# The modulation's three parts beside the first layer's attention: float32 products in four column groups of TensorE in place of sums on VectorE

## The chip, the core and the metric

The kernel runs on one core of one Trainium2 chip. Each run gives one device time in microseconds (us); the metric is that time, and 1309.29 us is the median of three runs before the change (1306.78 to 1309.57). A profile comes from one execution of its own, which took 1307.82 us; its span, from the first to the last instruction, is 1306.0 us. In the rows of the profile PE is TensorE's matmuls, PEld its weight loads, DVE is VectorE, ACT is ScalarE, POOL is GpSimd and SP is SyncE, which issues nearly all DMAs here.

## The reference

A decoder trunk of two layers over 512 positions of width 1024, all in float32. Each layer begins with a modulation: one row of 6144 numbers, the product of a conditioning vector of 1024 with a matrix of 1024 x 6144, plus a bias. It is split into six parts of 1024.

```
c_act = jax.nn.silu(c)
for i in range(DEPTH):
    mod = jnp.einsum('bd,dm->bm', c_act, w_mod[i]) + b_mod[i]
    sh_a, sc_a, gt_a, sh_f, sc_f, gt_f = jnp.split(mod, N_MOD, axis=-1)
    h = modulate(rmsnorm(x, g_mix_pre[i]), sh_a, sc_a)
    qkv = jnp.einsum('bsd,de->bse', h, w_qkv[i])
    ...
    o = jnp.einsum('bse,ed->bsd', merge_heads(o), w_o[i])
    x = x + gt_a[:, None, :] * rmsnorm(o, g_mix_post[i])
    h = modulate(rmsnorm(x, g_ffn_pre[i]), sh_f, sc_f)
    ...
    x = x + gt_f[:, None, :] * rmsnorm(y, g_ffn_post[i])
```

`modulate(h, shift, scale)` is `h * (1 + scale) + shift`; what is left out is the attention (stick-breaking in layer 0, forgetting in layer 1) and the gated MLP with its convolution. The change concerns three parts of layer 0: `gt_a` (in the code `GT_A`), `sc_f` (`SC_F`) and `sh_f` (`SH_F`). None is needed before the attention of layer 0 has ended.

## The kernel before

**Products.** TensorE's products of the model take fp32r operands, to which a float32 is rounded. To keep the precision, a helper splits each operand into a rounded high half and the rest (`split`, L191 to L193: a copy on ACT, a subtraction on DVE or POOL), and each product of the model is three matmuls: high x high, high x low, low x high (`mm3`, L264 to L268). Transpositions (L319, L422) are matmuls of plain float32 against an identity matrix, whose tile is named `zid`.

**The stages.** `begin` makes `sh_a` and `sc_a` of layer 0, normalises the input and makes the first projections, to about 72 us. Then `attention` runs over 16 heads and one round more. For each head TensorE makes four blocks of scores (`ps`, L388), ACT takes two sigmoids of each (L397, L398), DVE makes a running product (`om`, L399), DVE or POOL a product (`bt`, L400), TensorE transposes the result one head later (`pa`, L422), ACT and DVE split it (`ah`, `al`, L192, L193), and TensorE multiplies it by the values (`po`, L437, L438). Between these steps `fill` puts matmuls of the next heads' projections (`pqk`, `pv`), so many per head as the table `UNITS` says. After it comes the output projection with `postnorm`, which needs `GT_A`, and then the gated MLP with `SC_F` and `SH_F`.

**The order of the work.** TensorE and SP keep the order in which the program is written. DVE, ACT and POOL, after `begin`, are ordered by a scheduler before the run; on the chip every engine then works strictly in its order. SP runs ahead of the others and stops only where a buffer that a DMA is to fill is still in use.

**The three parts.** `mod_part` (L130) is a generator that `Background.step` advances a piece at a time; `attention` calls it at the end of each head from the third on, three pieces each (L567), with a priority that lets the scheduler place them early. For one part it loads eight blocks of 128 rows x 1024 columns of the matrix (`wm`, L139) and adds each on DVE, times the conditioning number of its row, to a sum of 128 x 1024 (`acc`; the first by L141, the others by L143, eight by L143 in `GT_A`, whose sum starts from the bias). The sum over the 128 rows is then made on TensorE: `acc` is split (L146, L148) and multiplied by a matrix of ones in four matmuls (L160, L161). For `GT_A` the result is multiplied by a weight vector (L163); for `SC_F` and `SH_F` the diagonal is taken out as columns by eight reductions on DVE (`diagonal`, L128). The conditioning vector lies in `csil`, 128 x 8.

The loads of `wm` go to three buffers of the tag `t4`, shared with other tiles of that size. `xn` is a tag with two buffers, used in `begin` and after the attention. PSUM has eight banks, all of one tag.

Of the kernel before, what the change touches and what calls it, by code (L numbers as in the profile page):

```python
# [8 lines left out]
F32 = mybir.dt.float32  # L9
# [3 lines left out]
ALU = mybir.AluOpType  # L13
AX = mybir.AxisListType

P = 128
D = 1024
S = 512
NT = S // P
ND = D // P  # L20
# [13 lines left out]
SH_A, SC_A, GT_A, SH_F, SC_F, GT_F = range(6)  # L34
# [3 lines left out]
def trunk(ctx, tc, x, c, w_mod, b_mod, g_mix_pre, g_mix_post, w_qkv, w_o, w_fg, b_fg,  # L38
          g_ffn_pre, g_ffn_post, w_gate, w_up, w_conv, b_conv, w_down, out):
    nc = tc.nc  # L40
    cst = ctx.enter_context(tc.tile_pool(name="cst", bufs=1))
    sb = ctx.enter_context(tc.tile_pool(name="sb", bufs=1))
# [4 lines left out]
    def nm(s):  # L47
        serial[0] += 1
        return f"{s}_{serial[0]}"

    def bank(s="b"):
        return pp.tile([P, 512], F32, tag="bank", name=nm(s), bufs=8)

    def slot(s, dt=F32R):
        return sb.tile([P, 512], dt, tag="slot", name=nm(s), bufs=NS)

    def t2(s):
        return sb.tile([P, 512], F32, tag="t2", name=nm(s), bufs=4)

    def t4(s, dt=F32):  # L60
        return sb.tile([P, D], dt, tag="t4", name=nm(s), bufs=3)
# [10 lines left out]
    idn = zid[:, S - P :]  # L72
# [3 lines left out]
    ones = cst.tile([P, P], F32R, name="ones")  # L76
# [9 lines left out]
    colB = [cst.tile([P, 88], F32, name=f"colB{l}") for l in range(DEPTH)]  # L86
    xs = cst.tile([P, NT, D], F32, name="xs")
    csil = cst.tile([P, ND], F32, name="csil")
    rowsA, rowsB, rowsC = t2("rowsA"), t2("rowsB"), t2("rowsC")
    nc.sync.dma_start(rowsC[:ND, :P], c.rearrange("b (r p) -> (b r) p", p=P))  # L90
    nc.scalar.dma_start(rowsA[:96, :P], b_mod.rearrange("l (r p) -> (l r) p", p=P))
# [3 lines left out]
    def b_col(l, comp):  # L95
        return colA[:, 48 * l + 8 * comp : 48 * l + 8 * comp + 8]

    def g_col(l, comp):
        o = (96 if comp == SC_A else 112) + 8 * l
        return colA[:, o : o + 8]  # L100

    def mod_columns():
        ps = bank("pcol")
        nc.tensor.transpose(ps[:, :ND], rowsC[:ND, :P], idn[:ND, :ND])
        nc.scalar.activation(csil, ps[:, :ND], AF.Sigmoid)
        nc.vector.tensor_tensor(csil, csil, ps[:, :ND], op=ALU.mult)
        nc.tensor.transpose(ps[:, 128:256], rowsA[:, :P], idn)
        nc.scalar.copy(colA, ps[:, 128:256])

# [14 lines left out]
    made = {}  # L124

    def diagonal(dst, src):

        nc.vector.tensor_tensor_reduce(junk(P), src, idn, 1.0, 0.0, op0=ALU.mult, op1=ALU.add, accum_out=dst)  # L128

    def mod_part(l, comp):  # L130
        row = comp in (GT_A, GT_F)
        acc = sb.tile([P, D], F32, tag="acc", name=nm("acc"), bufs=1)
        lo_c = comp * D
        if row:
            nc.gpsimd.memset(acc, 0.0)
            nc.sync.dma_start(acc[0:1, :], b_mod[l : l + 1, lo_c : lo_c + D])
        for d in range(ND):
            w = t4("wm")
            nc.sync.dma_start(w, w_mod[l, d * P : (d + 1) * P, lo_c : lo_c + D])  # L139
            if d == 0 and not row:  # L140
                nc.vector.tensor_scalar(acc, w, csil[:, 0:1], None, op0=ALU.mult)  # L141
            else:
                nc.vector.scalar_tensor_tensor(acc, w, csil[:, d : d + 1], acc, op0=ALU.mult, op1=ALU.add)  # L143
            yield
        ah = t4("ah", F32R)
        nc.scalar.copy(ah, acc)  # L146
        al = t4("al", F32R)
        nc.vector.tensor_tensor(al, acc, ah.bitcast(F32), op=ALU.subtract)  # L148
        if row:
            res = sb.tile([P, D], F32, tag="gt", name=nm("gt"), bufs=2)  # L150
            gp = t4("gp")
            g = (g_mix_post if comp == GT_A else g_ffn_post)[l]
            nc.sync.dma_start(gp, g.rearrange("(o n) -> o n", o=1).to_broadcast([P, D]))
        else:
            res = cst.tile([P, ND], F32, name=nm("mc"))
        yield
        for h in range(2):
            cs = slice(512 * h, 512 * h + 512)
            ps = bank("pm")
            nc.tensor.matmul(ps, ones, ah[:, cs], start=True, stop=False)  # L160
            nc.tensor.matmul(ps, ones, al[:, cs], start=False, stop=True)  # L161
            if row:
                nc.vector.tensor_tensor(res[:, cs], ps, gp[:, cs], op=ALU.mult)  # L163
            else:
                for j in range(4):
                    diagonal(res[:, 4 * h + j : 4 * h + j + 1], ps[:, j * P : (j + 1) * P])
            yield
        if not row:
            nc.vector.tensor_tensor(res, res, b_col(l, comp), op=ALU.add)
            if comp in (SC_A, SC_F):  # L170
                nc.vector.scalar_tensor_tensor(res, res, 1.0, g_col(l, comp), op0=ALU.add, op1=ALU.mult)
        made[l, comp] = res

    class Background:
        def __init__(self, parts):
            self.gens = [mod_part(*p) for p in parts]

        def step(self, n=1):
            while n and self.gens:
# [11 lines left out]
    def split(hi, lo, src, engine=None):  # L191
        nc.scalar.copy(hi, src)  # L192
        (engine or nc.vector).tensor_tensor(lo, src, hi.bitcast(F32), op=ALU.subtract)  # L193
# [189 lines left out]
    def scores(l, hd, qb, q, k):  # L383
        n = (qb + 1) * P
        qs = slice(qb * P, n)
        ps = bank("ps")
        for i in range(2):
            nc.tensor.matmul(ps[:, :n], q[hd][:, qs], k[hd][i][:, :n], start=i == 0, stop=i == 1)  # L388
        return ps, n
# [25 lines left out]
    def transposed(probs):  # L415

        res = {}
        for kb in range(NT):
            n = (NT - kb) * P
            ps = bank("pa")  # L420
            for qb in range(NT - 1, kb - 1, -1):
                nc.tensor.transpose(ps[:, (qb - kb) * P : (qb - kb + 1) * P], probs[qb][:, kb * P : (kb + 1) * P], idn)  # L422
            if kb == 1:
                shared = slot("ah"), slot("al")
            hi, lo = (slot("ah"), slot("al")) if kb in (0, 2) else shared
            o = 384 if kb == 3 else 0
            hi, lo = hi[:, o : o + n], lo[:, o : o + n]
            split(hi, lo, ps[:, :n])
            res[kb] = (hi, lo)
            yield res  # L430
# [92 lines left out]
    def drain(g):  # L523
        for _ in g:
            pass

    def attention(l, qk, vt, ot, filler, units, bg):


        get = cums_of.get(l)  # L530
        late, cums = None, {}
        for h in range(NH + 1):
            p, hd = divmod(h, 2)
            done = [0, 0]

            def fill(n=1):
                done[0] += n
                u = (units[h] * min(done[0], 12) + 11) // 12 - done[1]
                done[1] += u
                filler.run(u)  # L540

            if h < NH and hd == 0:
                ot.append((slot("oh"), slot("ol"), slot("of", F32)))
            if get and h < NH:
                for i in range(h, min(h + 2, NH)):
                    if i not in cums:
                        cums[i] = get(i)
            probs, at = {}, None
            turned = transposed(late[0]) if late else None
            for qb in range(NT - 1, -1, -1):  # L550
                if h < NH:
                    ps, n = scores(l, hd, qb, qk[p, 0], qk[p, 1])
                    probs[qb] = stick(ps, n) if l % 2 == 0 else fox(ps, qb, cums[h])
                    fill()
                if turned:
                    at = next(turned)
                    fill()
            fill(2)
            if late:
                drain(turned)  # L560
                for i, _ in enumerate(weighted(late[1], vt, at, ot[late[1] // 2])):
                    if i % 2:
                        fill()
            fill(12)
            late = (probs, h)
            with tc.high_priority(offset=-100):
                bg.step(3 if h > 1 else 0)  # L567


    def begin(vt, qk):  # L570
# [192 lines left out]

    cums_of = {}
    for l in range(DEPTH):
        bg = Background([(l, GT_A), (l, SC_F), (l, SH_F)] if l == 0 else [])
        scale = -0.125 if l % 2 else 0.125
        vt, qk, kl[:] = {}, {}, low_rooms()
        if l == 0:
# [38 lines left out]
        gens += [project(t, ps_) for ps_ in (range(3), range(3, 5)) for t in range(2)] + [project(2, range(3))]  # L808
        filler = Filler(gens)
        attention(l, qk, vt, ot, filler, UNITS[l], bg)  # L810
        filler.finish()
        bg.finish()
# [3 lines left out]
        xn = {}  # L816
# [22 lines left out]
        bg = Background([(l, GT_F)] + ([(l + 1, c_) for c_ in (SC_A, SH_A, SC_F, SH_F, GT_A)] if l + 1 < DEPTH else []))  # L839
# [33 lines left out]
        for f in range(2, NF):  # L873
            g, u = bank("pgu"), bank("pgu")
# [67 lines left out]
```

## Time and profile before

| | |
|---|---|
| median of three runs | 1309.29 us |
| the profiled execution, its span | 1307.82 us, 1306.0 us |
| TensorE's granted clock, mean | 0.989 |
| busy: PE, PEld, DVE, ACT, POOL | 1249.1, 1050.2, 818.9, 620.0, 277.2 us |
| first scores of layer 0, last weighted sum of its attention | 71.9 us, 271.3 us |
| DMAs of `wm` in the attention | 24 of 512 KB, 4.4 us to landing each |

A row of a stage (a window) gives the stretch, its length, the busy time of each engine with its number of instructions, the granted clock, the mean share of the DMA engines and GB/s. A row of a group gives line, engine, operation, the tile written and those read, the shapes and the count; then busy time and the mean of one in ns; then the idle time of the engine just before them and what ended it. The busy time of PE is made of matmuls that overlap, so it is not their cost: that is the distance between one start and the next.

### The profile page before, as it was taken

The numbers are of one execution on the slowest core, as the hardware profiler recorded it, in microseconds if no ns is written. First come the engines' busy times: TensorE is split into PE (matmuls) and PEld (weight loads), VectorE is DVE, ScalarE is ACT, GpSimd is POOL, SyncE is SP. The second block draws the span as 40 slices with busy tenths as digits, with TensorE's granted clock in tenths as the row PEclk, the third lists the DMA queues.
The fourth block names the chain that finished last, engine by engine and source line by source line (L and its number), as shares of the span: only waits on it lengthen the run. The fifth ranks groups of instructions, "written<-read, shape, count | busy, mean of one in ns | idle before, by whom it ended". The sixth has DMA issues, their size and how long they took to land.

```text
span 1306.0 us, 17087 instructions
## 1 busy us (share of the span) xinstructions
PE 1249.1 (96%) x6244; PEld 1050.2 (80%) x6244; DVE 818.9 (63%) x1447; ACT 620.0 (47%) x1182; POOL 277.2 (21%) x302
## 2 busy tenths in 40 slices
PE   5898988999999999999999899999999999999997
PEld 3676867789888888888887788887898888888886
DVE  7778888856878887422264776886775444443233
ACT  5576665757433333311365565566753333332121
POOL 3665444530000000000114554443100000000000
PEclk8999989999999999999999999999999999999999
DMA  8662534231577776333503423232263333333331
GB/s 265 208 193 82 168 107 133 94 108 43 189 242 242 246 229 202 97 97 97 164 1 115 130 91 120 81 129 81 66 210 113 97 97 98 97 97 97 97 97 65
DMA packets 174856, 169.19 MB, mean 130 GB/s; under 512 B 6936, under 2 KB 151728, under 8 KB 174772
## 3 DMA queue, kind: packets, MB, share of 16 engines
q1 hardware_dynamic: 174596, 168.04, 41.1%
q8 instruction: 49, 0.80, 0.3%
q14 instruction: 35, 0.29, 0.1%
q10 hardware_dynamic: 176, 0.07, 0.0%
HBM read 165.92 MB, written 2.16 MB: 129 GB/s over the span
## 4 chain that ended last, share of the span: by engine, by line
PE 72%; DVE 14%; ACT 5%; DMA 4%; issue 3%; POOL 1%; SPq 0%; DVEq 0%; POOLq 0%; ACTq 0%
PE pgu L267 11%; PE pgu L268 11%; PE pgu L266 11%; PE pd L268 6%; PE pd L267 6%; PE pd L266 6%; PE pqk L266 2%; DVE acc L143 2%; PE pqk L267 2%; PE pqk L268 2%; PE po L266 2%; PE po L268 2%; PE po L267 2%; PE ps L388 2%; DMA wm<-in_w_mod_dram 2%
## 5 line engine op out<-in xcount | busy, mean ns | idle before, releaser
L192 ACT CAST wh<-wf 128x1024 fp32r<-128x1024 f32 (+2 forms) x178 | 185.3, 1041 | 319.7 <-PE pgu L267 144.0
L193 DVE TENSOR_TENSOR wl<-wf,wh 128x1024 fp32r<-128x1024 f32 x122 | 149.3, 1224 | 217.9 <-ACT wh L192 215.7
L267 PE MATMUL pgu<-htl,wh 128*128 128x512 f32 (+1 forms) x736 | 276.4, 375 | 0.1
L266 PE MATMUL pgu<-hth,wh 128*128 128x512 f32 (+1 forms) x736 | 276.4, 375 | 0.0
L268 PE MATMUL pgu<-hth,wl 128*128 128x512 f32 (+1 forms) x736 | 276.2, 375 | 0.0
L193 POOL TENSOR_TENSOR wl<-wf,wh 128x1024 fp32r<-128x1024 f32 (+3 forms) x56 | 132.5, 2370 | 131.6 <-ACT wh L192 126.4
L267 PEld LDWEIGHTS pgu<-htl,wh 128*128 128x128 f32 x736 | 138.5, 188 | 25.6 <-DVE htl L328 0.5
L268 PEld LDWEIGHTS pgu<-hth,wl 128*128 128x128 f32 x736 | 138.5, 188 | 25.1
L266 PEld LDWEIGHTS pgu<-hth,wh 128*128 128x128 f32 x736 | 138.5, 188 | 24.9
L279 POOL TENSOR_TENSOR r<-v,mhalf 128x1 f32<-128x1 f32 x32 | 17.9, 558 | 447.3 <-DVE v L275 447.3
L266 PE MATMUL pd<-wh,yh 128*128 128x512 f32 x288 | 112.0, 389 | 0.0
L267 PE MATMUL pd<-wl,yh 128*128 128x512 f32 x288 | 112.0, 389 | 0.0
L268 PE MATMUL pd<-wh,yl 128*128 128x512 f32 x288 | 112.0, 389 | 0.0
L143 DVE SCALAR_TENSOR_TENSOR acc<-wm,csil,acc 128x1024 f32<-128x1024 f32 x74 | 99.4, 1344 | 17.1 <-DMA wm<-in_w_mod_dram 16.8
L266 PE MATMUL pqk<-hth,wh 128*128 128x512 f32 (+1 forms) x240 | 101.5, 423 | 0.1
L268 PE MATMUL pqk<-hth,wl 128*128 128x512 f32 (+1 forms) x240 | 94.5, 394 | 0.3 <-POOL wl L193 0.3
L267 PE MATMUL pqk<-htl,wh 128*128 128x512 f32 (+1 forms) x240 | 94.1, 392 | 0.0
L854 ACT ACTIVATE cv<-cv 128x512 f32<-128x512 f32 x44 | 27.8, 632 | 102.7 <-DVE cv L853 98.2
L266 PE MATMUL pv<-wh,hth 128*128 128x256 f32 (+1 forms) x224 | 70.7, 316 | 1.2 <-ACT wh L192 0.8
L267 PE MATMUL pv<-wl,hth 128*128 128x256 f32 (+1 forms) x224 | 67.7, 302 | 1.2 <-POOL wl L193 1.2
L268 PE MATMUL pv<-wh,htl 128*128 128x256 f32 (+1 forms) x224 | 67.9, 303 | 0.0
L266 PEld LDWEIGHTS pd<-wh,yh 128*128 128x128 f32 x288 | 54.1, 188 | 11.3
(194 smaller groups left out, 2459.6 us busy)
## 6 DMA issues: line engine op xcount, KB each, us to landing
wm<-in_w_mod_dram SPq DMA_DIRECT2D x80, 512.0 KB, 4.8
wf<-in_w_ffn_gate_dram SPq DMA_DIRECT2D x44, 512.0 KB, 4.2
wf<-in_w_ffn_up_dram SPq DMA_DIRECT2D x44, 512.0 KB, 3.7
wf<-in_w_ffn_down_dram SPq DMA_DIRECT2D x44, 512.0 KB, 3.5
wf<-in_w_qkv_dram SPq DMA_DIRECT2D x41, 512.0 KB, 3.8
wm<-in_w_mod_dram SPq DMA_DIRECT2D x32, 256.0 KB, 4.3
wf<-in_w_o_dram SPq DMA_DIRECT2D x16, 512.0 KB, 3.8
cum<-cumd SPq DMA_DIRECT2D x16, 512.0 KB, 4.3
```

The costliest lines, as they stand in the source:

```text
L143: nc.vector.scalar_tensor_tensor(acc, w, csil[:, d : d + 1], acc, op0=ALU.mult, op1=ALU.add)
L192: nc.scalar.copy(hi, src)
L193: (engine or nc.vector).tensor_tensor(lo, src, hi.bitcast(F32), op=ALU.subtract)
L266: nc.tensor.matmul(ps, ah, bh, start=first, stop=False)
L267: nc.tensor.matmul(ps, ah, bl, start=False, stop=False)
L268: nc.tensor.matmul(ps, al, bh, start=False, stop=last)
L279: nc.gpsimd.tensor_tensor(r, v, mhalf, op=ALU.pow)
L388: nc.tensor.matmul(ps[:, :n], q[hd][:, qs], k[hd][i][:, :n], start=i == 0, stop=i == 1)
L854: nc.scalar.activation(a, a, AF.Silu)
```

## The change

`mod_part` stays for layer 1 and for the parts that are made beside the MLP. The three parts beside layer 0's attention are made by a new generator, in halves of 512 columns. For one half:

- the eight blocks of 128 x 512 come in four DMAs of 512 KB, two blocks each, into two buffers of `t4` and two of `xn`; for `GT_A` also two rows, spread over all partitions, into a third `t4` (`gb`);
- eight matmuls of plain float32, each with a stationary operand of 128 x 32 (one column of `csil` in a tile `c32` whose other 31 columns are zero) and a moving one of 128 x 512; the d-th goes to columns 32 (d % 4) of the array and writes 32 partitions of one bank, two products onto each group of partitions;
- for `GT_A` the bank is split and summed over partitions by two matmuls with ones, then DVE adds the bias and multiplies by the weights; for the other two ACT copies the bank, four transpositions turn it, and one reduction on DVE adds the four groups.

`attention` now takes one step at the end of each head from the second on and one more in the middle of every second head, without the priority. So, counting heads from 0, the first loads are issued in head 1, the products stand at the end of head 2, and the rest in the middle of head 3; then the next half follows, and so on to head 13. `xn` and `t4` are free for a new half's loads once the products of the half before have read them.

```
+    c32 = cst.tile([P, ND, 32], F32, name="c32")
+    nc.gpsimd.memset(c32, 0.0)
...
+        nc.vector.tensor_copy(c32[:, :, 0:1], csil.unsqueeze(2))
...
+    def mod_part_pe(l, comp):
+        row = comp in (GT_A, GT_F)
...
+        for h in range(2):
+            c0 = comp * D + 512 * h
+            w = []
+            for i in range(4):
+                if i == 2:
+                    yield
+                w.append(t4("wm") if i % 2 else sb.tile([P, D], F32, tag="xn", name=nm("wm"), bufs=2))
+                nc.sync.dma_start(w[i].rearrange("p (d e) -> p d e", d=2),
+                                  w_mod[l].rearrange("(d p) e -> p d e", p=P)[:, 2 * i : 2 * i + 2, c0 : c0 + 512])
+            if row:
+                gb = t4("gb")
+                for o, v in ((0, g[512 * h : 512 * h + 512]), (512, b_mod[l, c0 : c0 + 512])):
+                    nc.sync.dma_start(gb[:, o : o + 512], v.rearrange("(o n) -> o n", o=1).to_broadcast([P, 512]))
+            yield
+            ps = bank("pm")
+            for d in range(ND):
+                q = 32 * (d % 4)
+                nc.tensor.matmul(ps[q : q + 32, :], c32[:, d, :], w[d // 2][:, 512 * (d % 2) : 512 * (d % 2) + 512],
+                                 start=d < 4, stop=d > 3, tile_position=(0, q))
+            if row:
+                a = slot("mh"), slot("ml")
+                split(*a, ps)
+            else:
+                f = slot("mf", F32)
+                nc.scalar.copy(f, ps)
+            yield
+            ps = bank("pm")
+            cs = slice(512 * h, 512 * h + 512)
+            if row:
+                for i in range(2):
+                    nc.tensor.matmul(ps, ones, a[i], start=i == 0, stop=i == 1)
+                nc.vector.tensor_tensor(res[:, cs], ps, gb[:, 512:], op=ALU.add)
+                nc.vector.tensor_tensor(res[:, cs], res[:, cs], gb[:, :512], op=ALU.mult)
+            else:
+                for j in range(4):
+                    nc.tensor.transpose(ps[:, j * P : (j + 1) * P], f[:, j * P : (j + 1) * P], idn)
+                nc.vector.tensor_reduce(res[:, 4 * h : 4 * h + 4], ps.rearrange("p (j q k) -> p j q k", q=4, k=32)[:, :, :, 0], axis=AX.X, op=ALU.add)
...
     class Background:
-        def __init__(self, parts):
-            self.gens = [mod_part(*p) for p in parts]
+        def __init__(self, parts, make=mod_part):
+            self.gens = [make(*p) for p in parts]
...
             fill(2)
+            if h % 2:
+                bg.step()
...
             late = (probs, h)
-            with tc.high_priority(offset=-100):
-                bg.step(3 if h > 1 else 0)
+            if h:
+                bg.step()
...
-        bg = Background([(l, GT_A), (l, SC_F), (l, SH_F)] if l == 0 else [])
+        bg = Background([(l, GT_A), (l, SC_F), (l, SH_F)] if l == 0 else [], mod_part_pe)
```

What stands on TensorE at the end of head 2 before the change: the last weighted sums of a head (`po`) and then the next head's first scores (`ps`).

```order
L437 MATMUL po_1135<-ah_1067,v_783 128x128
L438 MATMUL po_1135<-al_1068,v_783 128x128
L388 MATMUL ps_1163<-kh_882,qb_799 128x512
L388 MATMUL ps_1163<-kl_100,qb_799 128x512
L266 MATMUL pqk_1118<-hth_107,wh_891 128x512
```

And with the change, at the same place (`c_90` is the tile `c32`; x2 stands for two matmuls in a row):

```order
L491 MATMUL po_1150<-ah_1082,v_786 128x128
L492 MATMUL po_1150<-al_1083,v_786 128x128
L202 MATMUL pm_1166<-wm_1012,c_90 32x512 x2
L202 MATMUL pm_1166<-wm_1014,c_90 32x512 x2
L202 MATMUL pm_1166<-wm_1030,c_90 32x512 x2
L202 MATMUL pm_1166<-wm_1032,c_90 32x512 x2
L442 MATMUL ps_1179<-kh_885,qb_802 128x512
L442 MATMUL ps_1179<-kl_102,qb_802 128x512
```

The eight products of a half stand as one block between two heads, ahead of the scores on which the next head's chain on ACT and DVE rests; there are six such blocks.

On DVE, around the same head boundary, before the change: the end of a head (`of`, `ol`), sums of the part `GT_A` (L143), the next head's running products (`om`) and the splits of transposed blocks (`al`).

```order
L443 TENSOR_TENSOR of_811<-po_1135,of_811 64x512
L143 SCALAR_TENSOR_TENSOR acc_1151<-wm_1435,csil,acc_1151 128x1024
L193 TENSOR_TENSOR ol_810<-of_811,oh_809 128x512
L143 SCALAR_TENSOR_TENSOR acc_1151<-wm_1438,csil,acc_1151 128x1024
L399 SCALAR_TENSOR_TENSOR om_1167<-ps_1163,zid 128x512
L193 TENSOR_TENSOR al_1182<-pa_1176,ah_1181 128x512
L148 TENSOR_TENSOR al_1443<-acc_1151,ah_1441 128x1024
L399 SCALAR_TENSOR_TENSOR om_1192<-ps_1188,zid 128x384
```

With the change, at the same place:

```order
L497 TENSOR_TENSOR of_814<-po_1150,of_814 64x512
L247 TENSOR_TENSOR ol_813<-of_814,oh_812 128x512
L247 TENSOR_TENSOR ml_1176<-pm_1166,mh_1175 128x512
L453 SCALAR_TENSOR_TENSOR om_1183<-ps_1179,zid 128x512
L247 TENSOR_TENSOR al_1198<-pa_1192,ah_1197 128x512
L453 SCALAR_TENSOR_TENSOR om_1208<-ps_1204,zid 128x384
```

The two sums of 128 x 1024 and the subtraction of that size that stood among the head's own work are gone; one subtraction of 128 x 512 (`ml`) stands there instead.

On SP, the DMAs of heads 1 to 3 before the change (`wf` are weights of the projections):

```order
L198 DMA wf_1112<-in_w_qkv_dram 128x8x128
L136 DMA acc_1151<-in_b_mod_dram 1x1024
L139 DMA wm_1154<-in_w_mod_dram 128x1024
L139 DMA wm_1157<-in_w_mod_dram 128x1024
L139 DMA wm_1160<-in_w_mod_dram 128x1024
L198 DMA wf_1215<-in_w_qkv_dram 128x8x128
```

With the change:

```order
L192 DMA wm_1012<-in_w_mod_dram 128x2x512
L192 DMA wm_1014<-in_w_mod_dram 128x2x512
L192 DMA wm_1030<-in_w_mod_dram 128x2x512
L192 DMA wm_1032<-in_w_mod_dram 128x2x512
L197 DMA gb_1034<-in_g_mix_post_dram 128x512
L197 DMA gb_1034<-in_b_mod_dram 128x512
L252 DMA wf_1127<-in_w_qkv_dram 128x8x128
L252 DMA wf_1231<-in_w_qkv_dram 128x8x128
L192 DMA wm_1293<-in_w_mod_dram 128x2x512
```

The first half's six DMAs have moved ahead of a load of weights (`wf_1127`, before `wf_1112`), and the second half's first load (`wm_1293`) stands behind the weights of the head after.

More of the change, by code (lines that the diff above doesn't have):

```diff
@@ L172, in mod_part @@
         made[l, comp] = res
+    def mod_part_pe(l, comp):
+        row = comp in (GT_A, GT_F)
+        if row:
+            res = sb.tile([P, D], F32, tag="gt", name=nm("gt"), bufs=2)
+            g = (g_mix_post if comp == GT_A else g_ffn_post)[l]
+        else:
+            res = cst.tile([P, ND], F32, name=nm("mc"))
+        for h in range(2):
[26 more added lines that the diff above has]
+            cs = slice(512 * h, 512 * h + 512)
+            if row:
+                for i in range(2):
+                    nc.tensor.matmul(ps, ones, a[i], start=i == 0, stop=i == 1)
+                nc.vector.tensor_tensor(res[:, cs], ps, gb[:, 512:], op=ALU.add)
+                nc.vector.tensor_tensor(res[:, cs], res[:, cs], gb[:, :512], op=ALU.mult)
+            else:
+                for j in range(4):
+                    nc.tensor.transpose(ps[:, j * P : (j + 1) * P], f[:, j * P : (j + 1) * P], idn)
+                nc.vector.tensor_reduce(res[:, 4 * h : 4 * h + 4], ps.rearrange("p (j q k) -> p j q k", q=4, k=32)[:, :, :, 0], axis=AX.X, op=ALU.add)
+        if not row:
+            nc.vector.tensor_tensor(res, res, b_col(l, comp), op=ALU.add)
+            if comp in (SC_A, SC_F):
+                nc.vector.scalar_tensor_tensor(res, res, 1.0, g_col(l, comp), op0=ALU.add, op1=ALU.mult)
+        made[l, comp] = res
```

## The prediction

> **What bounds the kernel now.** I read the page first, then one table of stages, then who waits for whom in the one stage that the change touches.
>
> ```profile
> PE 1249.1 (96%) x6244; PEld 1050.2 (80%) x6244; DVE 818.9 (63%) x1447; ACT 620.0 (47%) x1182; POOL 277.2 (21%) x302
> ...
> PE 72%; DVE 14%; ACT 5%; DMA 4%; issue 3%; POOL 1%; SPq 0%; DVEq 0%; POOLq 0%; ACTq 0%
> ```
>
> TensorE is busy in 96% of the span and holds 72% of the chain that ended last. So a change can win where TensorE waits, and it loses wherever it gives TensorE more than that. The stage is layer 0's attention, 72 to 272 us. The windows of before, cut where the work of `mod_part` begins and ends:
>
> ```profile
> 72.00:90.00 18.00, 17.44 (x85) 13.74 (x84) 14.96 (x25) 15.80 (x36) 12.28 (x16) 1.00 0.70 222
> 90.00:122.00 32.00, 25.45 (x119) 20.12 (x120) 29.32 (x42) 16.30 (x34) 16.22 (x20) 0.95 0.42 131
> 122.00:144.00 22.00, 22.00 (x127) 18.94 (x126) 17.66 (x34) 17.27 (x37) 12.98 (x17) 1.00 0.00 1
> 144.00:160.00 16.00, 16.00 (x124) 15.49 (x123) 13.95 (x22) 9.61 (x22) 5.04 (x9) 1.00 0.85 274
> 160.00:170.00 10.00, 5.07 (x18) 3.62 (x18) 9.97 (x9) 3.54 (x10) 5.89 (x7) 0.75 0.72 246
> 170.00:200.00 30.00, 29.20 (x145) 23.67 (x144) 26.21 (x50) 20.95 (x45) 13.50 (x21) 0.97 0.33 97
> 200.00:226.00 26.00, 21.99 (x153) 20.62 (x152) 22.63 (x45) 14.07 (x33) 11.34 (x15) 0.93 0.39 133
> 226.00:236.00 10.00, 10.00 (x55) 8.47 (x54) 6.29 (x13) 8.53 (x18) 6.48 (x9) 1.00 0.34 105
> 236.00:272.00 36.00, 34.26 (x184) 28.41 (x183) 27.33 (x62) 25.34 (x58) 21.14 (x30) 1.00 0.29 89
> 72.00:272.00 200.00, 181.41 (x999) 153.09 (x998) 168.31 (x294) 131.43 (x287) 104.87 (x138) 0.97 0.40 128
> ```
>
> The same windows for line 143 alone, the sums on DVE:
>
> ```profile
> 90.00:122.00 32.00, 10.27 (x6) 0.95 0.42 131
> 122.00:144.00 22.00, 0.00 (x0) 1.00 0.00 1
> ...
> 160.00:170.00 10.00, 3.93 (x3) 0.75 0.72 246
> 170.00:200.00 30.00, 5.10 (x4) 0.97 0.33 97
> 200.00:226.00 26.00, 5.78 (x5) 0.93 0.39 133
> 226.00:236.00 10.00, 0.00 (x0) 1.00 0.34 105
> ```
>
> TensorE stands idle for 200 - 181.4 = 18.6 us. In the four stretches 90 to 122, 160 to 170, 170 to 200 and 200 to 226 it is 6.6 + 4.9 + 0.8 + 4.0 = 16.3 us, and there the granted clock falls too (0.95, 0.75, 0.97, 0.93). In 122 to 144 and 226 to 236, where no such sum runs, TensorE is never idle at a clock of 1.00. Who is waited for, in 72 to 272:
>
> ```profile
> PE ps L388 <- DVE om L399: 12.4, 6, 4.9
> PE pa L422 <- DVE om L399: 2.5, 2, 1.4
> PE po L438 <- DVE al L193: 1.8, 3, 1.0
> PE ps L388 <- POOL kh L379: 0.8, 1, 0.8
> PE ps L388 <- DVE v L193: 0.3, 1, 0.3
> PE po L437 <- DVE om L399: 0.2, 1, 0.2
> ```
>
> 12.4 + 2.5 + 1.8 + 0.3 + 0.2 = 17.2 us of waits are for DVE: the scores wait for a running product (`om`) to release its bank, and that one queues behind a sum.
>
> **What goes from DVE.** Its groups in 72 to 272:
>
> ```profile
> L143 DVE SCALAR_TENSOR_TENSOR acc<-wm,csil,acc 128x1024 f32<-128x1024 f32 x22 | 32.8, 1491 | 5.7 <-DMA wm<-in_w_mod_dram 5.7
> L193 DVE TENSOR_TENSOR al<-pa,ah 128x512 fp32r<-128x512 f32 x16 | 10.7, 670 | 0.1
> L128 DVE CUSTOM_DVE_ANT_0 junk<-pm,zid 128x128 bf16<-128x128 f32 x16 | 4.6, 286 | 0.4
> L148 DVE TENSOR_TENSOR al<-acc,ah 128x1024 fp32r<-128x1024 f32 x3 | 4.3, 1445 | 1.4 <-ACT ah L146 1.4
> L141 DVE TENSOR_SCALAR acc<-wm,csil 128x1024 f32<-128x1024 f32 x2 | 1.7, 868 | 0.0
> L163 DVE TENSOR_TENSOR gt<-pm,gp 128x512 f32<-128x512 f32 x2 | 1.4, 682 | 0.5 <-PE pm L161 0.5
> L128 DVE DVE_READ_ACCUMULATOR2_ANT mc<- 128x1 f32 x16 | 1.3, 82 | 0.0
> ```
>
> Removed: 32.8 + 4.6 + 4.3 + 1.7 + 1.4 + 1.3 = 46.1 us, and 5.7 us in which DVE's queue stood still for a DMA of `wm`. Added: two subtractions of 128 x 512 at 0.67 us, four operations of that size in `gt` at 0.68, four reductions of 16 numbers a row at no more than a diagonal's 0.29: 5.2 us. DVE falls from 168 to about 127 us of the 200.
>
> What this returns to TensorE: at least the 17.2 us of waits seen, at most all idle time and all lost clock, 18.6 + 200 x 0.03 = 24.6 us. I take **23**, since the stretches free of sums are idle for 2.3 us (0.6 before 90, 1.7 after 236) that stay partly. On ACT three copies of 128 x 1024 give way to six of 128 x 512 from PSUM, much the same.
>
> **What comes to TensorE.** Three rows price it. They are the steady MLP stage, the chain's piece of eight float32 transpositions of 128 columns, and the busy time of a matmul and of a weight load:
>
> ```profile
> 520.00:600.00 80.00, 80.00 (x354) 66.24 (x354) 27.79 (x30) 20.75 (x24) 0.00 (x0) 1.00 0.31 94
> ...
> 290.45 0.87 PE pt L319 x8
> ...
> L267 PE MATMUL pgu<-htl,wh 128*128 128x512 f32 (+1 forms) x736 | 276.4, 375 | 0.1
> ...
> L267 PEld LDWEIGHTS pgu<-htl,wh 128*128 128x128 f32 x736 | 138.5, 188 | 25.6 <-DVE htl L328 0.5
> ```
>
> An fp32r matmul of 512 columns costs 80/354 = 0.226 us. Twelve go (three parts, four each) and four come: -1.8. Sixteen transpositions come at 0.87/8 = 0.109: +1.7. Net -0.1 us.
>
> The 48 float32 products of 512 columns are the disputed term: no row shows one, nor two matmuls side by side. From below, one pass of 0.226 us and four groups fully side by side: 12 x 0.226 = 2.7 us. From above, four passes, since the kernel's own split makes three products and drops low x low: 0.904 us each, one after another 43.4 us. The nearest row, a float32 transposition, is 0.109 us per 128 columns where fp32r pays 0.226/4 = 0.057: two passes, 48 x 0.436 = 20.9 us one after another. I take four passes in which a product overlaps only its neighbour, by half: TensorE starts matmuls in program order, the neighbour sits in another group, and the one after next must wait. A block of eight is then 9 halves of 0.452 us = 4.1 us, six blocks **24.4 us**, near the nearest row.
>
> The Trainium skill, "FP8 and Floating Point Precision", TensorE Precision Notes, gives true float32 four passes through the array; that would be the upper price per product, and no run here shows it.
>
> Going to column groups and back, 12 times, might also empty the array: a matmul lasts 0.375 us where the next starts after 0.226, so 0.15 us of tail, and a weight load of 0.19 us that no longer hides, 0.34 us, between 0 and 4.1 us. I take 0 and keep 4.1 for the range. The Trainium skill says in "TensorEngine Tiling (Array Packing)", Key Properties, that a change of the tiling mode drains TensorE; by that rule the sum would be up to 4.1 us higher, and nothing in this trace changes that mode in mid-stream.
>
> **Cover for the rest.** The blocks hold up the next head's scores, but all that time is TensorE's own and is counted above. In `begin`, DVE gets a small copy ahead of the first sum, which waits for its DMA anyway:
>
> ```profile
> 5.22 0.49 DVE L619 TENSOR_SCALAR pm<-wm,csil 128x256 f32<-128x256 f32 x1 [1.36 <-DMA wm<-in_w_mod_dram]
> ```
>
> 1.36 us of idle time hide it; without that cover it would cost its own 0.2 us. The memset of `c32` on POOL takes the place of a larger one (`kl`). The DMAs are as before, 24 of 512 KB:
>
> ```profile
> wm<-in_w_mod_dram SPq DMA_DIRECT2D x24, 512.0 KB, 4.4
> ```
>
> They land in 4.4 us and stand a whole head (10 us) ahead of their products. New is that SP waits at a half's first `wm` until the block before it has run on TensorE. Behind it queue the loads of `wf`, two projection tiles of 24 matmuls (5.4 us each) ahead of their use, so 11 us cover the landing and the split; a head without that cover would lose some 5 us.
>
> **The sum.** -23 - 0.1 + 24.4 = +1.3 us: 1309.1 us against the profiled execution's 1307.82. The median of the runs is 1.5 us above that one, so 1310.6 us against 1309.29. A difference of 0.2% (2.6 us) is about what a measurement of this kernel can tell from no change. With returns of 17.2 to 24.6 us and products of 20.9 to 28.5 (24.4 and the emptying) this case itself spans 1305.5 to 1320.5.
>
> **Rivals.** *Four wide (faster).* All four groups run side by side through all passes: 43.4/4 = 10.8 us, so 1309.3 - 23.1 + 10.8 = 1297.0. For it: the four groups write different partitions and read different tiles. Against it: passes of one product share a group, and starts are in order. It decides once more than two products overlap on average. The Trainium skill, "TensorE: Matmul & The Clock Gate", Measured speedup vs the span model, gives 2.38 times for three column groups; carried to four as an estimate, 3.2 times, that is 13.7 us and 1299.9, though its mechanism keeps matmuls in order. No run here shows either.
>
> *One after another (slower).* No overlap: 43.4 us, 1329.6. For it: in no row of this trace do two matmuls share the array. It overtakes the return as soon as a product costs over 23/48 = 0.48 us.
>
> *The wait moves (slower).* Only the scores' wait for `om` returns, 12.4 us, since a head's end still goes through ACT and DVE in turn: 1309.3 - 12.5 + 24.4 = 1321.2. Against it: 122 to 144 shows two heads with that same chain and no idle time.
>
> **How the numbers follow.** Forecast 0.45, four wide 0.25, one after another 0.23, the wait moves 0.07. The forecast's 0.45 falls into 0.12 faster, 0.18 within 0.2% and 0.15 slower. So faster 0.12 + 0.25 = 0.37, same 0.18, slower 0.15 + 0.23 + 0.07 = 0.45. The range goes from 1296 to 1330: it takes in both outer cases' own times and leaves out the far half of each.
>
> **What would show it.** The block of `pm<-wm,c32` between two heads: 4.1 us long if right, 1.8 if four wide, 7.2 if one after another. PE's waits for DVE in the stage near zero and the clock at 1.00, if the return is right; DVE at 127 us there. A wait of PE for `pm` on a DMA, or of `pqk` on `wl`, would show that the queue of SP was mispriced. The prediction is wrong if TensorE's idle time stays above 6 us, or the blocks last under 3 or over 5 us.

## The result

The changed kernel takes **1297.24 us** (median of four runs, 1295.95 to 1298.38), the kernel before, beside it on the same chip, 1308.03 (four runs, 1306.59 to 1309.57). The ratio is 0.991, with a 95% interval of 0.9893 to 0.9928: faster by 0.9%. The prediction was 1310.6, no change. The time lies in its range and on the number of the rival *four wide*, 1297.0.

### The profile page after: what moved, and what is told of

It is laid out like the page before. It is cut to its first block, busy times and chain, and to the rows that moved or that the text cites. A ratio compares the mean times of both kernels' runs of the same rounds, so it can differ in the third digit from the quotient of the medians.

```text
span 1296.6 us, 17226 instructions
## 1 busy us (share of the span) xinstructions
PE 1254.0 (97%) x6348; PEld 1050.5 (81%) x6348; DVE 783.0 (60%) x1397; ACT 621.3 (48%) x1185; POOL 269.8 (21%) x302
## 4 chain that ended last, share of the span: by engine, by line
PE 80%; DVE 9%; ACT 4%; DMA 3%; issue 2%; SPq 1%; POOL 1%; POOLq 0%; DVEq 0%; ACTq 0%
PE pgu L321 12%; PE pgu L322 12%; PE pgu L320 12%; PE pd L321 6%; PE pd L322 6%; PE pd L320 6%; PE pqk L320 3%; PE pqk L321 3%; PE pqk L322 3%; PE ps L442 3%; PE pa L476 2%; PE pv L320 2%; PE pv L321 2%; PE pv L322 2%; DVE fx L466 2%
## 5 line engine op out<-in xcount | busy, mean ns | idle before, releaser
L146 DVE SCALAR_TENSOR_TENSOR acc<-wm,csil,acc 128x1024 f32<-128x1024 f32 x52 | 66.6, 1280 | 12.4 <-DMA wm<-in_w_mod_dram 12.1
```

## The profile after

The profiled execution, the slowest of the four runs, took 1298.38 us; its span is 1296.6. First the busy times and the shares of the chain that ended last, of the changed kernel:

```profile
PE 1254.0 (97%) x6348; PEld 1050.5 (81%) x6348; DVE 783.0 (60%) x1397; ACT 621.3 (48%) x1185; POOL 269.8 (21%) x302
...
PE 80%; DVE 9%; ACT 4%; DMA 3%; issue 2%; SPq 1%; POOL 1%; POOLq 0%; DVEq 0%; ACTq 0%
```

TensorE's part of the chain rose from 72 to 80%, DVE's fell from 14 to 9%. The windows of the changed kernel at four cuts of before, and then from its first scores of layer 0 to the last weighted sum (columns as before):

```profile
90.00:122.00 32.00, 32.00 (x178) 25.77 (x177) 21.75 (x38) 20.03 (x42) 12.49 (x19) 1.00 0.37 123
160.00:170.00 10.00, 10.00 (x57) 8.47 (x56) 5.28 (x10) 6.68 (x14) 5.50 (x9) 1.00 0.32 104
200.00:226.00 26.00, 26.00 (x178) 22.45 (x177) 15.64 (x31) 18.44 (x40) 11.39 (x15) 1.00 0.57 201
72.00:272.00 200.00, 196.90 (x1157) 162.21 (x1156) 136.54 (x248) 138.57 (x301) 99.29 (x140) 1.00 0.40 132
...
71.00:258.10 187.10, 184.00 (x1100) 151.56 (x1099) 131.29 (x242) 132.36 (x290) 97.20 (x137) 1.00 0.43 140
```

In the three stretches where TensorE stood idle for 6.6, 4.9 and 4.0 us it is never idle now; in the whole stage it is idle for 3.1 us in place of 18.6, and the granted clock is 1.00. The attention lasts 187.1 us; before it was 199.4 (71.9 to 271.3). Who is waited for in 72 to 272 (us in total, times, the longest in us):

```profile
PE po L491 <- DVE om L453: 1.2, 1, 1.2
PE ps L442 <- DVE om L453: 0.7, 1, 0.7
PE ps L442 <- POOL kh L433: 0.4, 1, 0.4
PE po L492 <- DVE al L247: 0.3, 1, 0.3
PE ps L442 <- DVE v L247: 0.3, 1, 0.3
```

Of 17.2 us of waits for DVE 2.5 are left. The disputed block, the eight products at the end of head 2, in the timelines of PE and of PEld (start, time, engine, line, operation; equal neighbours are put together, x16):

```profile
100.12 0.27 PE L492 MATMUL po<-al,v 128*128 128x128 f32 x1
100.33 1.92 PE L202 MATMUL pm<-wm,c 128*32 128x512 f32 x16
102.18 0.50 PE L442 MATMUL ps<-kh,qb 128*128 128x512 f32 x1
...
100.33 0.16 PEld L202 LDWEIGHTS pm<-wm,c 128*32 128x32 f32 x8
100.78 0.13 PEld L202 LDWEIGHTS pm<-wm,c 128*32 128x32 f32 x4 [0.30 <-issue]
101.21 0.13 PEld L202 LDWEIGHTS pm<-wm,c 128*32 128x32 f32 x4 [0.30 <-issue]
```

A product stands in the trace as two matmuls. The loads show the rhythm: two rounds' weights at once, then four more as each round frees its groups, so there are four rounds of four, 0.43 us apart. From the first product to the next scores it is 102.18 - 100.33 = 1.85 us; predicted were 4.1 for the forecast, 1.8 for *four wide* and 7.2 for *one after another*.

The gain of the attention isn't kept whole. The first product of the MLP of layer 0 (`pgu`) is a good mark, since all that the change touches lies ahead of it; its row gives the first and the last start of all 736, over both layers. Before, then the change:

```profile
L266 PE MATMUL pgu<-hth,wh x736: 277/389/402, 303.0 to 1178.4; 128*128 128x512 f32 x160, 128*128 128x256 f32 x24
```

```profile
L320 PE MATMUL pgu<-hth,wh x736: 277/389/396, 289.8 to 1169.2; 128*128 128x512 f32 x160, 128*128 128x256 f32 x24
```

At the mark the change is 13.2 us ahead, at the last of them 9.2. Some 4 us go in a part of the program that the diff doesn't touch; where, is said below.

## Experiments on the products

The reading after the result, theory A in the texts on record: each group of columns takes its own products, whatever their order, so eight of them take two products' time; the block stands wholly on TensorE's path; and what pays for it is DVE's time. Each kernel below ran in turns with the kernel before, which had medians from 1308.2 to 1310.3 in the four series. A lead of one kernel of this part over another is taken between two series, so a us or two of it can be chance.

**All products in one group of columns** (`e1_one`).

```
-  nc.tensor.matmul(ps[q : q + 32, :], ..., start=d < 4, stop=d > 3, tile_position=(0, q))
+  nc.tensor.matmul(ps[:32, :], ..., start=d == 0, stop=d == ND - 1, tile_position=(0, 0))
```

> The changed kernel with all eight products of a half in one column group (32 partitions), so that only 32 partitions are copied, summed and transposed. Theory A (the gain is the column groups working side by side): a product then costs its two matmuls of 0.43 us in turn, a block 16 x 0.43 = 6.9 us where it takes 1.9 us now; six blocks add about 30 us, 1327 us. Rival B (the block is cheap for another reason, such as the 32-column stationary operand, and the groups matter little): within 3 us of the changed kernel, 1297 to 1300 us.

Measured: 1329.8 us, ratio 1.0161 (1.0113 to 1.021). The same block in its timeline:

```profile
101.20 7.05 PE L201 MATMUL pm<-wm,c 128*32 128x512 f32 x16
108.18 0.50 PE L441 MATMUL ps<-kh,qb 128*128 128x512 f32 x1
```

6.98 us for 16 matmuls of one group in a row, 0.436 each, so a product costs 0.87 us. That is the upper price of the prediction (0.904), and the time is that of its rival *one after another* (1329.6). The split into column groups is worth 32.6 us.

**Two groups of 64 columns** (`e2_two`): `c32` 64 columns wide, `q = 64 * (d % 2)`.

> The changed kernel with two column groups of 64 in place of four of 32 (c32 has 64 columns, of which 63 are zero; the tile onesf lies in another pool to make room). Theory A (as many products side by side as there are groups): a block is 8 x 0.43 = 3.4 us and its two edges, about 1.6 us more than with four; six add 10 us, 1307 us. Rival B (only neighbours in program order overlap, so that two groups do as well as four): 1297 us, blocks of 1.9 us.

Measured: 1306.92 us, ratio 0.9986 (0.9963 to 1.0009): within 0.2% of before. Its block:

```profile
100.93 3.65 PE L202 MATMUL pm<-wm,c 128*64 128x512 f32 x16
104.51 0.50 PE L442 MATMUL ps<-kh,qb 128*128 128x512 f32 x1
```

3.58 us. With 6.98, 3.58 and 1.85 us for one, two and four groups the block goes as the inverse of their number, and six blocks move the time with it.

**Another program order** (`e3_order`).

```
-            for d in range(ND):
+            for d in (0, 4, 1, 5, 2, 6, 3, 7):
```

> The changed kernel with the products of a half in the order 0 4 1 5 2 6 3 7, so that two products in a row go to the same column group. Theory A (each group takes its own matmuls as they come, whatever stands between in program order): blocks of about 1.9 us, 1297 us. Rival B (matmuls start in program order, and the four groups only overlap where the next matmul goes to a free one): a product waits for the one before it in its group, blocks of 3.5 us or more, 1307 us or more.

Measured: 1296.5 us, ratio 0.9913 (0.988 to 0.9945), as the change. Each product here stands right behind one of its own group. Were starts bound to the program's order, product 1 could not start before 4, which waits 0.87 us for 0, and so on: 5 products' times, 4.4 us. The block:

```profile
99.70 1.94 PE L202 MATMUL pm<-wm,c 128*32 128x512 f32 x16
101.57 0.50 PE L442 MATMUL ps<-kh,qb 128*128 128x512 f32 x1
```

1.87 us. The rows don't name the group of a matmul, so the time decides: a matmul to a free group starts ahead of one that waits for a busy group. The starts bear it out: four matmuls start at nearly the same time in each round, one every 13 ns here and one every 7 ns in the change, as if the one between them were passed over. The Trainium skill, "TensorE: Matmul & The Clock Gate", Part 3: Packing small matmuls, says that matmuls start and end strictly in order; for these, of two records a product, the measurement is against it.

**Each product made twice** (`e7_twice`): 16 products per half in place of 8.

> The changed kernel with each of the eight products of a half made twice (the three parts are then computed from twice the product, so they differ). Theory A (a block lies wholly on TensorE's path, four side by side): eight more products are four more slots of 0.43 us, 1.72 us a block, 10.3 us in all, 1307.5 us. Rival E (a block fills time in which TensorE would wait for the head's chain anyway): under 1302 us.

Measured: 1309.35 us, ratio 1.0 (0.998 to 1.0019), 12.1 us over the change. The block measures 106.29 - 102.72 = 3.57 us in its timeline, 1.72 more, six times 10.3. From the first scores of layer 0 to the mark it is 302.4 - 73.4 = 229.0 us against 289.8 - 71.0 = 218.8, 10.2 more. So no cover hides the block: what it grows by is on the path.

**One part by sums again** (`e10_mixed`): `SH_F` by `mod_part`, the other two as in the change.

> The changed kernel with the third part (SH_F) made by sums on VectorE again, one step at a time over heads 9 to 15, and the other two by products. Theory A: two blocks of 1.97 us and eight transpositions go from TensorE, 4.8 us less, but four matmuls with ones (0.9 us) come back and VectorE's sums bring waits again; if these few sums find room 1293 us, if a sum costs here what it cost before (24 us over 22 sums, some 8 us for a third) 1301 us. Rival E (blocks are covered): 1297 us or more.

Measured: 1303.85 us, ratio 0.9957 (0.994 to 0.9973), 6.6 us over the change for one of three parts, and 2.9 over the dearer of theory A's two figures. One part back on DVE gives back 6.6 of the 10.8 us that the change won. So this mixture doesn't help; no other was run.

## Experiments on what DVE gives back

**The priority of the background work** (`e6_noprio`), which the change also drops: the kernel before without `high_priority`.

> The kernel before without the priority of the background's steps, the sums left on VectorE. Theory A (the time of the sums and their waits count, not their rank with the scheduler): 1303 to 1313 us. Rival C (the sums hurt because they are placed early and ahead of the head's own work; dropping the priority is the gain): 1300 us or less.

Measured: 1310.39 us, ratio 1.0005 (0.9986 to 1.0023). Dropping the priority is worth nothing by itself that these runs can tell.

**Short sums** (`e5_nosums`): in the kernel before, the sums of L143 cover 16 of 1024 columns (`n = 16`, written out here).

```
-  nc.vector.scalar_tensor_tensor(acc, w, csil[:, d : d + 1], acc, ...)
+  nc.vector.scalar_tensor_tensor(acc[:, :16], w[:, :16], csil[:, d : d + 1], acc[:, :16], ...)
```

> The kernel before, where the sums of the three parts beside layer 0's attention cover 16 of their 1024 columns (the other columns of those three parts are left out; loads, waits and everything behind the sums stay). Theory A (what the change wins is TensorE's wait for a late VectorE, about 24 us, and it pays some 12 us of it for products): without the sums and without products about 1284 us, TensorE's idle time in the attention under 5 us. Rival C (the gain comes from the order and the placement of the steps, not from VectorE's time): 1303 us or more.

Measured: 1300.13 us, ratio 0.9922 (0.9894 to 0.9949): a miss of theory A by 16 us. The group of the sums on DVE says why in two numbers:

```profile
L143 DVE SCALAR_TENSOR_TENSOR acc<-wm,csil,acc 128x16 f32<-128x16 f32 x22 | 12.9, 587 | 11.4 <-DMA wm<-in_w_mod_dram 11.0
```

They still last 587 ns on the mean, not the 0.22 to 0.24 us that 12 of the 22 take, and DVE stands still in front of them for 11.0 us until a load has landed. The runs after the next one take these waits away.

**Only the loads** (`e9_loads`): the kernel before with the loads of `wm` kept, and no sums, splits, matmuls or diagonals of the three parts.

> The kernel before, where nothing of the three parts beside layer 0's attention is computed: their loads stay, nothing reads them, and the results are filled with ones (all sums, their summing over partitions and the columns of these three parts are left out). The run with sums of 16 columns kept 11 us of waits of VectorE's queue for those loads. Theory A (a sum costs its time and, standing in VectorE's strict order, also its wait for the load; both together are what the change gives back): no such wait, TensorE idle under 3 us in the attention, 1283 us (1297.2 less six blocks of 1.97 us and 2.6 us of summing and turning). Rival D (the attention's own chain limits it as soon as the sums are shorter): about 1300 us, as with sums of 16 columns.

Measured: 1281.75 us, ratio 0.9801 (0.9772 to 0.9831). Its mark and its window:

```profile
L277 PE MATMUL pgu<-hth,wh x736: 277/389/396, 274.9 to 1150.6; 128*128 128x512 f32 x160, 128*128 128x256 f32 x24
```

```profile
72.00:272.00 200.00, 197.53 (x1118) 169.99 (x1117) 142.91 (x258) 144.68 (x324) 102.28 (x144) 1.00 0.42 139
```

From the first scores of layer 0 (at 71.9, 71.0 and 71.7 us in before, the change and this kernel) to the mark it is 231.1, 218.8 and 203.2 us, and that parts the two halves of the change. The old way cost 231.1 - 203.2 = 27.9 us, of which twelve matmuls at 0.226 are 2.7: the rest of the three parts' work, DVE's above all and three copies on ACT, with its waits, held TensorE up for **25.2 us**. The new way costs 218.8 - 203.2 = 15.6 us: six blocks of 1.85 are 11.1, four matmuls and sixteen transpositions 2.6, and 1.9 us are left, 0.3 a block. Net of these the change returns 23.3.

**The waits for loads** (`e11_resident`, `e12_short`): the sums read the resident `xs` in place of `wm`, over all 1024 columns and over 16; the loads stay.

```
+  nc.vector.scalar_tensor_tensor(acc[:, : n or D], (xs[:, d % 4, :] if n else w)[:, : n or D], ...)
```

In the next two texts A means that the waits in DVE's queue are dearer than the sums.

> The kernel before, in which the sums of the three parts read the resident input xs in place of the loaded blocks wm; the loads are still issued, but nothing reads them, so the three parts hold other numbers. The sums keep their full 1024 columns, only DVE's wait for the loads is gone. Theory A (a wait of DVE's queue for a load holds up all that stands behind it, and is dearer than the sums' own time): most of the way from before, 1308, to the kernel with loads alone, 1282; 1290, between 1286 and 1296. Rival B (the sums and the other work of the parts on DVE are the cost, the waits are small, 5.7 us seen): 1302 to 1308.

> As the other kernel of this call, and the sums cover 16 of 1024 columns, as in the earlier kernel with short sums (1300.1), which still waited for its loads. Theory A: without the waits 1285 (1282 with loads alone, 2.7 for the twelve matmuls with ones), between 1283 and 1290. Rival B (what is left on DVE there, the splits and the diagonals, is the cost): 1297 to 1300.

Measured: 1317.65 us with full sums, ratio 1.0065 (1.0045 to 1.0085), and 1298.11 with short ones, ratio 0.9905 (0.9887 to 0.9923). That theory falls: without the waits the full sums are slower, and the short ones are 2 us ahead of those that waited, less than these runs can tell from nothing. In the first the scheduler, with no load to wait for, also puts the sums ahead of other work on DVE (TensorE's waits for `al` ahead of `po` rise to 11.5 us), so its loss is that of placing and of time together, which these runs don't part.

From the first scores to the mark it is 231.1 us before, 222.0 with short sums, 219.7 with short sums that wait for nothing and 203.2 with loads alone. So the length of the sums is worth 9 of the 27.9 us, and 16.5 go only with the rest: the short sums themselves, the splits, the twelve matmuls (2.7) and the diagonals. Which of these weighs most no run here shows. One way in which a short step is dear is seen in the second kernel's timeline, DVE first, then POOL and PE:

```profile
109.39 2.26 DVE L143 SCALAR_TENSOR_TENSOR acc<-xs,csil,acc 128x16 f32<-128x16 f32 x1
111.57 0.68 DVE L193 TENSOR_TENSOR al<-pa,ah 128x512 fp32r<-128x512 f32 x1
...
109.28 2.34 POOL L193 TENSOR_TENSOR wl<-wf,wh 128x1024 fp32r<-128x1024 f32 x1
112.30 0.47 PE L422 MATMUL pa<-zid,bt 128*128 128x128 f32 x1 [2.98 <-DVE al L193]
```

A sum of 0.235 us that began 0.1 us after a subtraction on POOL ended with it, at 111.6, and TensorE waited 2.98 us for the `al` queued behind it. The same pair stands in the kernel before, with a wait of 3.27 us behind it:

```profile
111.05 2.76 POOL L193 TENSOR_TENSOR wl<-wf,wh 128x1024 fp32r<-128x1024 f32 x1 [4.01 <-ACT wh L192]
111.51 3.39 DVE L143 SCALAR_TENSOR_TENSOR acc<-wm,csil,acc 128x1024 f32<-128x1024 f32 x1
116.21 0.33 PE L388 MATMUL ps<-kh,qb 128*128 128x128 f32 x1 [3.27 <-DVE om L399]
```

The Trainium skill, "SBUF — State Buffer", Who interferes with whom, states this: an instruction of DVE with two inputs in SBUF and one of GpSimd that reads SBUF exclude each other, and the later waits for the whole of the earlier. These rows agree with it, with 2.26 us in place of 0.235.

**POOL's subtractions in four pieces** (`e13_quarters` on the kernel before, `e14_quarters` on the changed one).

```
+  if engine is not None and list(src.shape) == [P, 1024]:
+      for k in range(0, 1024, 256):
+          engine.tensor_tensor(lo[:, k : k + 256], src[:, k : k + 256], hi[:, k : k + 256].bitcast(F32), op=ALU.subtract)
+  else:
...
```

> The kernel before, with each of POOL's subtractions of 128x1024 (the low halves of the projections' weights) made in four pieces of 256 columns. In the profile of before a sum on DVE that began while POOL ran such a subtraction (2.40 us) ended only about a sum's own time after POOL's end (3.39 us in place of 1.28, with TensorE waiting 3.27 us behind it). Theory P (POOL's long operations hold up DVE's operations with two operands from SBUF, and part of what the change returns is this): a hold lasts at most one piece, 0.6 us, and 3 to 6 us return: 1303 to 1306. Rival (such holds hit where DVE has time, or the pieces follow so closely that DVE gets in no sooner): 1307 to 1311.

> The changed kernel with the same subtractions in four pieces. Theory P: with the sums gone from DVE there is little left to hold up, so 0 to 2 us return: 1295 to 1297. Rival: 1297 to 1299, no difference, or more if the pieces' own costs on POOL come onto the path.

Measured: 1299.36 us, ratio 0.9924 (0.9909 to 0.9938), and **1289.55 us**, ratio 0.9848 (0.9833 to 0.9863): the second beats both kernels. Both gain more than theory P said, and elsewhere. From the first scores to the mark nothing is gained: 230.8 us against 231.1, and 218.7 against 218.8. The gain is in layer 1's attention, from its first scores to the mark of its MLP: 230.9 us before, 234.5 in the change, 225.4 and 223.0 with pieces. There DVE scales 64 blocks of `fx` (one tile as input, where the sums have two). The changed kernel, then the one with pieces; before, these 64 took 48.3 us as well:

```profile
L466 DVE TENSOR_SCALAR fx<-fx,rc 128x512 f32<-128x512 f32 (+1 forms) x64 | 48.3, 755 | 1.0
```

```profile
L470 DVE TENSOR_SCALAR fx<-fx,rc 128x512 f32<-128x512 f32 (+1 forms) x64 | 32.5, 508 | 1.0
```

15.8 us less on DVE for the same 64 instructions. In the changed kernel the eleven scalings of 128 columns beside which POOL does nothing take 0.28 to 0.29 us, the five beside such a subtraction 1.37 to 2.24. So POOL's long subtractions do hold DVE up, but in layer 0 no time comes back by shortening them, and theory P is right of the mechanism and wrong of the place.

## Why the prediction was wrong

**The products, 24.4 us taken, about 11 measured: this step failed.** It said that "a product overlaps only its neighbour, by half: TensorE starts matmuls in program order". The price of one was right (0.87 us against 0.904). The order doesn't bind across groups: `e3_order` sets it against the overlap and loses nothing, and one, two and four groups give 6.98, 3.58 and 1.85 us. So "every engine then works strictly in its order", as it is put ahead of the prediction, doesn't hold for TensorE's products in different column groups. The sum said 1.3 us more than the profiled execution of before, and the span came out 9.4 less. Of these 10.7 us the products are 24.4 - 11.1 = 13.3; the return, 25.2 in place of 23, adds 2.2, and the stage's earlier start 0.9; the 1.9 left over at the blocks and the 3.8 given back later (below) take off 5.7.

**The choice by the nearest row** misled too: 20.9 us, one after another at two passes, lay near the 24.4, and that was taken as support. Both were wrong: a product takes 0.87 us, twice that row's 0.436, and four run at once, so the same 48 cost 20.9 x 2 / 4 = 10.5 us.

**The return, 23 us: right in size.** It is 25.2, a little over the upper bound of 24.6, and 23.3 net of the 1.9 left over at the blocks. The 17.2 us of waits seen stood for nearly half as much again, the lost clock among it. That a running product "queues behind a sum" is only part of how it came about: the length of the sums is worth 9 us, and the rest of the parts' work more.

**DVE at 127 us: nearly.** 131.3 us within the attention against 168.4, and 136.5 against 168.3 in 72 to 272.

**Emptying the array, 0 to 4.1 us, taken 0:** at most 2.6 us, the 1.9 left over and six times the 0.11 by which a block of 1.85 exceeds two products' 6.98 / 4 = 1.74. The Trainium skill, "TensorEngine Tiling (Array Packing)", Key Properties, has a change of the tiling mode drain TensorE; that agrees with some such cost, here at most 0.4 us a block.

**SP's wait: as predicted.** It waits 82.1 us in seven pieces for the products before, and no wait of TensorE in the stage is for `pm`, `wl` or a load.

**The rivals.** *Four wide* was the case, at its own time. *The wait moves* falls with the idle time of 3.1 us in 72 to 272.

**Not foreseen: 3.8 us given back after the mark** (1306.0 - 303.0 = 1003.0 us to the end of the span, now 1296.6 - 289.8 = 1006.8). 3.6 of them are in layer 1's attention, whose code is the same. Its window, before and then the change:

```profile
704.60:935.50 230.90, 222.05 (x1248) 190.09 (x1249) 167.99 (x418) 141.90 (x335) 102.97 (x85) 0.99 0.37 115
```

```profile
691.80:926.30 234.50, 224.93 (x1248) 192.67 (x1249) 168.38 (x418) 142.19 (x335) 103.10 (x85) 0.98 0.36 113
```

DVE and POOL are as busy as before, and TensorE is idle for 9.6 us in place of 8.9. The other 2.9 us are TensorE's own: the same 1248 matmuls are busy for 224.9 us in place of 222.0, at a granted clock of 0.98 in place of 0.99. The trace's record of the clock has three stretches of 3.4 us at half the clock in this window, where before had one. With POOL's subtractions in pieces the window falls to 225.4 us with one such stretch and to 223.0 with none. `e2_two` and `e7_twice`, which have the change with other products, take 231.6 with one. So the 3.6 us hang on how TensorE's stops fall, and the new way of making the parts doesn't bring them by itself; what shifted the stops stays open.

## What to carry to other kernels

Float32 products whose result needs only a few columns can share TensorE in four column groups at about a quarter of their time, in both orders tried here; price them so before trading them against an engine that TensorE waits for. Ask what a slow instruction on an off-path engine queues behind it, and what it locks out: a subtraction of 2.3 us on POOL made a 0.2 us step of DVE into one of 2.3 us, and four pieces in place of one were worth 0.6% on top of the change. A return read from waits alone was too low here, 17.2 us against 25.2, since the clock fell with them.

## What the hardware showed

Short stops can cost TensorE more than their length. In layer 1 of the changed kernel three stops of 0.27, 0.70 and 0.73 us lie within 3 us (timeline of PE):

```profile
822.90 0.38 PE L492 MATMUL po<-al,v 128*128 128x256 f32 x1 [0.27 <-DVE al L247]
823.99 0.33 PE L491 MATMUL po<-ah,v 128*128 128x128 f32 x1 [0.70 <-ACT ah L246]
825.05 0.33 PE L492 MATMUL po<-al,v 128*128 128x128 f32 x1 [0.73 <-DVE al L247]
825.21 0.45 PE L320 MATMUL pqk<-hth,wh 128*128 128x512 f32 x1
825.50 0.57 PE L321 MATMUL pqk<-htl,wh 128*128 128x512 f32 x1
825.87 0.63 PE L322 MATMUL pqk<-hth,wl 128*128 128x512 f32 x1
826.29 0.63 PE L442 MATMUL ps<-kh,qa 128*128 128x512 f32 x1
826.72 0.63 PE L442 MATMUL ps<-kl,qa 128*128 128x512 f32 x1
...
828.43 0.87 PE L476 MATMUL pa<-zid,fx 128*128 128x128 f32 x4
829.05 0.36 PE L320 MATMUL pv<-wh,hth 128*128 128x256 f32 x1
```

From 825.5 to about 829 a matmul of 512 columns starts every 0.43 us in place of 0.23. For the seven such matmuls from 825.5 to 828.4 that is 7 x 0.2 = 1.4 us on top of the stops. The trace's record of the clock has it at one half from 825.56 for 3.41 us. The stretches of 3.41 us around it:

```profile
822.15:825.56 3.41, 1.70 (x8) 1.00 (x7) 2.93 (x9) 0.91 (x4) 0.22 (x1) 1.00 0.37 118
825.56:828.97 3.41, 3.41 (x11) 2.63 (x10) 1.38 (x3) 1.13 (x2) 1.43 (x2) 0.50 0.94 299
828.97:832.38 3.41, 3.41 (x30) 3.41 (x29) 2.27 (x3) 3.21 (x7) 2.89 (x2) 1.00 0.13 49
```

TensorE is idle for 1.71 us of the first, half of it. In the 14 profiles of this case, from 32 us on and up to the last 8 us, every fall to half comes behind such a stretch with 1.44 us of idle time or more, 36 times, and no stretch at full clock with over 1.73 us of idle time went without one. The Trainium skill, "TensorE: Matmul & The Clock Gate", What's actually happening, tells of such a half rate in windows of about 3.4 us, and the 3.41 us agree; that it comes after an idle window these rows don't bear out as it stands, since about half a window of idle time, in stops of 0.73 us at most, was enough.
